# Norms at the boundaries of a two-block transformer kernel, and its last gate by token tiles

## The chip, the cores and the metric

The kernel runs on one core of a Trainium2 chip. The metric is the device time of one execution, in microseconds (us). The engines are TensorE (PE in the profile; PEld is its weight load), VectorE (DVE), ScalarE (ACT), GpSimd (POOL) and SyncE (SP), which issues most of the DMA transfers. Each engine works through its own instructions in order; semaphores tie the engines together.

## The reference

Two models in a row work on 512 tokens of width 1024, all in float32. The first has two layers, each with a mixer and a feed-forward network; a norm stands ahead of each of them and another on what it gives:

```python
h = x
for layer in range(2):
    xn = _rms_norm(h, norm_g[layer, 0])
    m = _even_mixer(xn, ...) if layer == 0 else _sgu_mixer(xn, ...)
    h = h + _rms_norm(m, norm_g[layer, 1])
    f = _squared_relu_mlp(_rms_norm(h, norm_g[layer, 2]), ffn_w1[layer], ffn_w2[layer])
    h = h + _rms_norm(f, norm_g[layer, 3])
```

with `_rms_norm(x, g) = x * rsqrt(mean(x * x) + eps) * g`, the mean over the 1024 columns of a token. The second model is one block whose shifts, scales and gates (`mod`) come from a condition vector: a norm, a scale and a shift, an attention mixer, a gate, `h = h + gate * mixer`; then a norm, a scale and a shift, a SwiGLU network, a gate, `h = h + gate * swiglu`; and a final norm with weights of its own. The kernel returns that.

## The kernel before

The residual stream `h` lies in SBUF with a token on each partition: four token tiles `i` of 128 tokens, 1024 columns each. The input `x` of a product lies the other way round, with features on the partitions, so between two blocks the tokens have to be normed and turned by TensorE (`fl`, L560, four 128x128 transposes into one PSUM bank). A float32 product is made of three matmuls (`mm3`, L275): every operand is split into a high part rounded to the matmul's format and the low part that is left (for weights L265 on ACT gives `whi` and L266 on DVE gives `wlo`, 1024 columns at a time).

There are five boundaries, near 319 us (even mixer to first feed-forward), 683 (first feed-forward to gMLP mixer), 964 (gMLP to second feed-forward), 1326 (second feed-forward to attention) and 1699 (attention to SwiGLU). `boundary` (L588) weaves three streams together on TensorE: `tail`, the last matmuls of the old block, token tile by token tile in two halves `c` of 512 columns; `bridge` or `shifted`, which turn two token tiles (half 0 is tiles 0 and 1, half 1 is tiles 2 and 3); and `head`, the first matmuls of the new block. The table `PLACES` (L229) says after how many steps of `tail(2)`, `tail(3)`, `head(0)` and `head(1)` which half is turned: an entry is (steps, half).

`norm_evac` (L530) is what follows each tail bank at the first four boundaries: `m` plus the bank on DVE (L540; a copy on ACT, L542, at the first), its sum of squares on ACT (L492, `ssm`), the product with the norm's weights on POOL (L544, in place), and after the second half the inverse root (L502 on DVE, L503 on POOL, `rsm`) and `h` (L548 on DVE, 1024 columns). `normed` (L523) then takes the sum of squares of the new `h` (`ssh`) and its inverse root (`col`). `bridge` evacuates unscaled transposes (L486 on ACT, L487 on DVE), and a later product applies the root; its broadcast over the partitions is `rb`. `shifted`, at the last two boundaries, needs the scaled token, since a shift is added: there L528 on ACT writes `h` times its root to another tile, that tile is turned, and for each of eight feature blocks ACT (L584) writes the high part of `x` from PSUM, DVE (L583) the whole value, and DVE (L585) the low part.

The SwiGLU network (L1593) runs in six hidden groups. `fi(g)` computes group `g`; `accum_group` (L1169) multiplies group `g-1` by its part of the output weights and adds the result to `m`, in eight banks, all four token tiles of `c` = 0 and then those of `c` = 1. After the loop the gate's row is made (`mod_row`, L511: matmuls `mrow` and copies on ACT), and POOL multiplies `m` by it (L1622) and adds it to `h` (L1623). The sixth group is the final tail: for each of its eight banks (`l`) DVE multiplies by the row (L1628, into `m`) and adds to `h` (L1629), ACT squares, POOL multiplies by the final norm's weights (L1631, into `m`), and after the second half of a tile the inverse root and the scaled output follow (DVE's half is L1637), and its transfer. A PSUM tag has two banks (`g`, `o`) or four (`s`). A Tile scheduler sets the order in which an engine gets its instructions, by priority and readiness.

## Time and profile before

| | |
|---|---|
| times of three runs | 2090.65, 2093.2, 2094.97 us (median 2093.2) |
| profiled execution | 2088.22 us, its span 2086.4 us |
| mean granted TensorE clock | 0.986 |
| TensorE busy | 2029.1 us (97%) |
| DVE, ACT, POOL busy | 53%, 39%, 9% |

The profile shows one execution. The span runs from its first to its last instruction. A busy TensorE is not a TensorE at full speed: its granted clock is one of two levels, 2.4 GHz (1.00) and 1.2 GHz (0.50), and a stretch's mean lies between them. Time in which an engine stands idle is put down to what released it, "idle before <- releaser".

### The profile page before, as it was taken

What the parts mean: (1) busy time and instruction counts of PE and PEld (TensorE: products, weight loads), DVE (VectorE), ACT (ScalarE), POOL (GpSimd) and SP (SyncE); (2) the same over time, 40 slices, a digit from 0 to 9 for tenths busy, and PEclk for the clock granted to TensorE, in tenths of its full rate; (3) what the DMA queues carried; (4) which work ended last, traced back from release to release, by engine and by line L of the source; (5) the groups of instructions that cost most, each with busy time, mean ns of one, the idle gap of its engine ahead of it and who ended that gap; (6) DMA issues with size and microseconds to landing.
All of it is one profiled execution on the core that took longest, in us unless ns stands there. A gap on an engine that the chain in (4) does not pass through costs nothing.

```text
span 2086.4 us, 25962 instructions
## 1 busy us (share of the span) xinstructions
PE 2029.1 (97%) x10296; PEld 1713.9 (82%) x10296; DVE 1110.1 (53%) x1682; ACT 810.9 (39%) x1356; POOL 184.0 (9%) x222
## 2 busy tenths in 40 slices
PE   8989999999999999999999999899999999999996
PEld 6867889888888788888888888898888888888885
DVE  7676646666665446665444444633563664334333
ACT  5455555322334443224523223534755344322221
POOL 3212230000002000003000000200000000000006
PEclk9989999999999999999999999999999999999998
DMA  7201044755542323221332233132122223232311
GB/s 250 84 31 41 31 154 125 241 190 195 178 144 68 125 89 100 89 90 61 121 101 91 91 101 101 51 102 71 60 73 65 77 92 119 93 101 92 100 61 41
DMA packets 59690, 213.54 MB, mean 102 GB/s; under 512 B 6951, under 2 KB 7272, under 8 KB 59184
## 3 DMA queue, kind: packets, MB, share of 16 engines
q1 hardware_dynamic: 56592, 202.84, 30.0%
q0 software_dynamic: 1728, 5.28, 0.9%
q10 hardware_dynamic: 1248, 3.76, 0.6%
q8 instruction: 81, 1.33, 0.3%
q14 instruction: 41, 0.34, 0.0%
HBM read 206.59 MB, written 2.10 MB: 100 GB/s over the span
## 4 chain that ended last, share of the span: by engine, by line
PE 77%; POOL 3%; DVE 3%; issue 2%; ACT 2%; POOLq 0%; ACTq 0%
PE g L278 12%; PE g L280 12%; PE g L279 12%; PE a L280 7%; PE a L279 7%; PE a L278 7%; PE h L279 2%; PE h L278 2%; PE h L280 2%; PE t L278 2%; PE t L279 2%; PE t L280 2%; POOL a L544 1%; PE l L278 1%; PE l L280 1%
## 5 line engine op out<-in xcount | busy, mean ns | idle before, releaser
L265 ACT CAST whi<-wraw 128x1024 fp32r<-128x1024 f32 x326 | 340.8, 1047 | 853.0 <-PE g L279 385.3
L266 DVE TENSOR_TENSOR wlo<-wraw,whi 128x1024 fp32r<-128x1024 f32 x326 | 399.3, 1228 | 312.9 <-ACT whi L265 309.5
L278 PE MATMUL g<-a,whi 128*128 128x512 f32 x1200 | 473.4, 395 | 0.0
L280 PE MATMUL g<-a,wlo 128*128 128x512 f32 x1200 | 470.1, 392 | 0.0
L279 PE MATMUL g<-a,whi 128*128 128x512 f32 x1200 | 469.8, 392 | 0.0
L278 PE MATMUL a<-whi,a 128*128 128x512 f32 x688 | 268.2, 390 | 0.0
L279 PE MATMUL a<-wlo,a 128*128 128x512 f32 x688 | 267.7, 389 | 0.0
L280 PE MATMUL a<-whi,a 128*128 128x512 f32 x688 | 267.7, 389 | 0.0
L280 PEld LDWEIGHTS g<-a,wlo 128*128 128x128 f32 x1200 | 225.9, 188 | 46.6
L278 PEld LDWEIGHTS g<-a,whi 128*128 128x128 f32 x1200 | 226.3, 189 | 45.4 <-DVE a L1575 0.2
L279 PEld LDWEIGHTS g<-a,whi 128*128 128x128 f32 x1200 | 226.2, 188 | 45.4
L1182 DVE TENSOR_TENSOR a<-a,a 128x512 f32<-128x512 f32 x168 | 114.6, 684 | 107.0 <-PE a L280 106.5
L279 PEld LDWEIGHTS a<-wlo,a 128*128 128x128 f32 x688 | 129.2, 188 | 26.8
L280 PEld LDWEIGHTS a<-whi,a 128*128 128x128 f32 x688 | 129.1, 188 | 26.7
L278 PEld LDWEIGHTS a<-whi,a 128*128 128x128 f32 x688 | 129.2, 188 | 26.5
L278 PE MATMUL h<-a,whi 128*128 128x256 f32 x384 | 108.6, 289 | 8.6 <-ACT a L584 5.2
L279 PE MATMUL h<-a,whi 128*128 128x256 f32 x384 | 109.1, 285 | 1.1 <-DVE a L585 1.1
L280 PE MATMUL h<-a,wlo 128*128 128x256 f32 x384 | 108.3, 284 | 0.0
L278 PE MATMUL l<-whi,a 128*128 128x512 f32 x256 | 101.6, 397 | 6.1 <-DVE a L1628 6.1
L1150 DVE SCALAR_TENSOR_TENSOR r<-g,rbc 128x512 f32<-128x512 f32 x52 | 35.9, 691 | 129.1 <-PE g L280 129.1
L280 PE MATMUL l<-whi,a 128*128 128x512 f32 x256 | 100.5, 393 | 0.0
L279 PE MATMUL l<-wlo,a 128*128 128x512 f32 x256 | 100.5, 393 | 0.0
(411 smaller groups left out, 2797.6 us busy)
## 6 DMA issues: line engine op xcount, KB each, us to landing
wraw<-wbig SPq DMA_DIRECT2D x320, 512.0 KB, 3.6
wada<-wada SPq DMA_DIRECT2D x48, 512.0 KB, 4.4
cw<-cmp_w SPq DMA_DIRECT2D x2, 1024.0 KB, 10.3
rowng<-rows POOLq DMA_DIRECT2D x4, 512.0 KB, 5.5
h<-x ACTq DMA_DIRECT2D x1, 2048.0 KB, 11.7
out<-a SPq DMA_DIRECT2D x8, 256.0 KB, 2.1
xin<-xT SPq DMA_DIRECT2D x3, 512.0 KB, 7.8
qt<-qt ACTq DMA_DIRECT2D x12, 128.0 KB, 2.3
```

Of the source, the lines that this page charges most:

```text
L265: nc.scalar.copy(hi[:, :w], raw)
L266: nc.vector.tensor_tensor(lo[:, :w], raw, hi[:, :w].bitcast(F32), ALU.subtract)
L278: mm(out, s[0], m[0], start=start, stop=False)
L279: mm(out, s[0], m[1], start=False, stop=False)
L280: self.gemm = mm(out, s[1], m[0], start=False, stop=stop).ins
L544: nc.gpsimd.tensor_tensor(t, t, g[:, c * 512:c * 512 + 512], ALU.mult)
L1150: done = nc.vector.scalar_tensor_tensor(r, o, 0.0, rb, ALU.max, ALU.mult).ins
L1182: nc.vector.tensor_add(t, t, o)
```

## The change

1. `norm_evac`: the product with the norm's weights of the second half (`c` = 1) goes to a tile of its own, `mg`, with a raised scheduling priority, where it was made in place; the update of `h` becomes two instructions of 512 columns.
2. `shifted`: the unscaled `h` is turned; L528 is gone. The inverse root is broadcast over the partitions by two small matmuls (`rb`) and copied to SBUF by ACT (`shb`). For each feature block DVE multiplies the transposed values by the weight and by `shb`, ACT adds the shift and writes the high part, DVE writes the low part; each reads what the one before it wrote. The first three of a half's four transposes are issued ahead of the broadcast, the fourth later.
3. `PLACES`: the gMLP boundary and the two shifted ones have other numbers.
4. The last gate: 16 products and 16 sums of 512 columns on POOL (`gated`) follow the accumulation of the last `accum_group`, bank by bank. The gate's row is made before `fi(0)`.

```diff
 PLACES = {
-    "norm": ((), ((2, 0),), ((18, 1), (34, 0)), ((20, 1),)),
-    "shifted": ((), ((12, 0),), ((27, 1),), ()),
+    "ffn": ((), ((2, 0),), ((18, 1), (34, 0)), ((20, 1),)),
+    "sgu": ((), ((2, 0),), ((23, 1), (30, 0)), ((20, 1),)),
+    "shifted": ((), ((0, 0), (7, 0), (14, 0)), ((16, 1), (25, 1), (40, 1)), ()),
 }
...
         self.factor(st["col"][:, i:i + 1], st["ssh"][:, i:i + 1])
-        if st["src"] is not self.h:
-            self.nc.scalar.activation(st["src"][:, i], self.h[:, i], AF.Copy, scale=st["col"][:, i:i + 1])
...
             self.square_sum(ss[:, 2 * i + c:2 * i + c + 1], t)
-            nc.gpsimd.tensor_tensor(t, t, g[:, c * 512:c * 512 + 512], ALU.mult)
             if c:
+                with self.tc.high_priority(URGENT):
+                    mg = self.rows.tile([P, 512], F32, tag="mg", name="mg", bufs=2)
+                    nc.gpsimd.tensor_tensor(mg, t, g[:, 512:], ALU.mult)
                 self.factor(rs[:, i:i + 1], ss[:, 2 * i:2 * i + 1], ss[:, 2 * i + 1:2 * i + 2])
-                h = self.h[:, i]
-                nc.vector.scalar_tensor_tensor(h, m[:, i], rs[:, i:i + 1], h, ALU.mult, ALU.add)
+                for k, t in enumerate((m[:, i, :512], mg)):
+                    h = self.h[:, i, 512 * k:512 * k + 512]
+                    nc.vector.scalar_tensor_tensor(h, t, rs[:, i:i + 1], h, ALU.mult, ALU.add)
                 self.normed(st, i)
+            else:
+                nc.gpsimd.tensor_tensor(t, t, g[:, :512], ALU.mult)
...
-        for k, o in self.flipped(st, half):
+        first = list(self.flipped(half, 0, 6))
+        yield
+        o = self.bank(self.ps, "rb", "s")
+        self.col_to_bc(o[:, :256], st["col"][:, 2 * half:2 * half + 2])
+        b = self.rows.tile([P, 256], F32, tag="shb", name="shb")
+        nc.scalar.copy(b, o[:, :256])
+
+        def evac(k, o):
             s = self.mod[:, sh * 8 + k:sh * 8 + k + 1]
             t = self.rows.tile([P, 256], F32, tag="sh", name="sh", bufs=2)
-            nc.vector.tensor_scalar(t, o, g[:, k:k + 1], s, ALU.mult, ALU.add)
-            nc.scalar.activation(x[0][:, k, t0:t1], o, AF.Identity, bias=s, scale=g[:, k:k + 1])
-            nc.vector.tensor_tensor(x[1][:, k, t0:t1], t, x[0][:, k, t0:t1].bitcast(F32), ALU.subtract)
+            nc.vector.scalar_tensor_tensor(t, o, g[:, k:k + 1], b, ALU.mult, ALU.mult)
+            nc.scalar.activation(x[0][:, k, t0:t1], t, AF.Identity, bias=s)
+            nc.vector.scalar_tensor_tensor(x[1][:, k, t0:t1], t, s, x[0][:, k, t0:t1].bitcast(F32), ALU.add, ALU.subtract)
+
+        for k, o in first:
+            evac(k, o)
+        yield
+        for k, o in self.flipped(half, 6, KD):
+            evac(k, o)
         yield
...
+            row, fin = self.mod_row(40, wk), self.row("nfin")
+
+            def gated(i, c):
+                cs = slice(c * 512, c * 512 + 512)
+                nc.gpsimd.tensor_tensor(m[:, i, cs], m[:, i, cs], row[:, cs], ALU.mult)
+                nc.gpsimd.tensor_tensor(self.h[:, i, cs], self.h[:, i, cs], m[:, i, cs], ALU.add)
+
             y = fi(0)
             for g in range(1, 6):
                 yn = fi(g)
-                self.accum_group("fo", y, m, g == 1)
+                self.accum_group("fo", y, m, g == 1, gated if g == 5 else None)
                 y = yn
-            row, fin = self.mod_row(40, wk), self.row("nfin")
             ss, col = self.cols4("ssm"), self.cols4("col")
-            for i in range(NT):
-                nc.gpsimd.tensor_tensor(m[:, i], m[:, i], row, ALU.mult)
-                nc.gpsimd.tensor_tensor(self.h[:, i], self.h[:, i], m[:, i], ALU.add)
```

`accum_group` calls `then(i, c)` behind each of its adds. Line numbers in the changed kernel are larger by 2 to 20.

On POOL, the end of the program: the gate's products and sums, the final norm's products (L1631), and its inverse roots (L503). Before:

```order
177 L1622 TENSOR_TENSOR a_13957<-a_13957,row_15872 128x1024 x2
178 L1623 TENSOR_TENSOR h<-h,a_13957 128x1024 x2
179 L1622 TENSOR_TENSOR a_13957<-a_13957,row_15872 128x1024 x2
180 L1623 TENSOR_TENSOR h<-h,a_13957 128x1024 x2
181 L1631 TENSOR_TENSOR a_13957<-h,rownfin 128x512
```

After (the last pairs of sixteen operations alike):

```order
202 L1638 TENSOR_TENSOR a_14001<-a_14001,row_14002 128x512
203 L1639 TENSOR_TENSOR h<-h,a_14001 128x512
204 L1638 TENSOR_TENSOR a_14001<-a_14001,row_14002 128x512
205 L1639 TENSOR_TENSOR h<-h,a_14001 128x512
206 L1653 TENSOR_TENSOR a_14001<-h,rownfin 128x512 x2
```

Product and sum alternate, one pair for each bank of 512 columns, and the final norm's first two products stand behind the last pair.

On POOL, the last token tiles at the gMLP boundary: L544, and after the change L554 (`c` = 0) and L547 (`c` = 1), are the products with the norm's weights, L503 and L505 the roots, L508 and L510 the transfer of a later norm's weights. Before:

```order
138 L544 TENSOR_TENSOR a_3530<-a_3530,rowng_5615 128x512 x2
139 L503 TENSOR_TENSOR rsm<-fa,mhalf 128x1
140 L503 TENSOR_TENSOR col<-fa,mhalf 128x1
141 L544 TENSOR_TENSOR a_3530<-a_3530,rowng_5615 128x512 x2
142 L508 DMA rowng_7695<-rows 128x1024
143 L503 TENSOR_TENSOR rsm<-fa,mhalf 128x1
144 L503 TENSOR_TENSOR col<-fa,mhalf 128x1
```

After:

```order
141 L554 TENSOR_TENSOR a_3538<-a_3538,rowng_5623 128x512
142 L547 TENSOR_TENSOR mg<-a_3538,rowng_5623 128x512
143 L505 TENSOR_TENSOR rsm<-fa,mhalf 128x1
144 L505 TENSOR_TENSOR col<-fa,mhalf 128x1
145 L547 TENSOR_TENSOR mg<-a_3538,rowng_5623 128x512
146 L554 TENSOR_TENSOR a_3538<-a_3538,rowng_5623 128x512
147 L510 DMA rowng_7711<-rows 128x1024
148 L505 TENSOR_TENSOR rsm<-fa,mhalf 128x1
149 L505 TENSOR_TENSOR col<-fa,mhalf 128x1
```

For the last token tile the product of `c` = 1 now stands ahead of that of `c` = 0, and the root behind both.

On DVE, the same place: from the update of `h` for the third token tile (L548, L551) over the evacuation of the first half's transposes (L487, L489) to the adds of the last token tile's two banks (L540). Before:

```order
623 L548 SCALAR_TENSOR_TENSOR h<-a_3530,rsm,h 128x1024
624 L487 SCALAR_TENSOR_TENSOR a_5654<-fl_95_5789,vecs,a_5653 128x256
625 L487 SCALAR_TENSOR_TENSOR a_5654<-fl_95_5798,vecs,a_5653 128x256
626 L487 SCALAR_TENSOR_TENSOR a_5654<-fl_95_5807,vecs,a_5653 128x256
627 L487 SCALAR_TENSOR_TENSOR a_5654<-fl_95_5816,vecs,a_5653 128x256
628 L540 TENSOR_TENSOR a_3530<-a_3530,l_95_5785 128x512
629 L500 TENSOR_SCALAR fa<-ssh 128x1
630 L487 SCALAR_TENSOR_TENSOR a_5654<-fl_95_5798,vecs,a_5653 128x256
631 L487 SCALAR_TENSOR_TENSOR a_5654<-fl_95_5807,vecs,a_5653 128x256
632 L487 SCALAR_TENSOR_TENSOR a_5654<-fl_95_5816,vecs,a_5653 128x256
633 L540 TENSOR_TENSOR a_3530<-a_3530,l_95_5838 128x512
```

After:

```order
629 L551 SCALAR_TENSOR_TENSOR h<-mg,rsm,h 128x512
630 L489 SCALAR_TENSOR_TENSOR a_5662<-fl_95_5803,vecs,a_5661 128x256
631 L489 SCALAR_TENSOR_TENSOR a_5662<-fl_95_5812,vecs,a_5661 128x256
632 L489 SCALAR_TENSOR_TENSOR a_5662<-fl_95_5821,vecs,a_5661 128x256
633 L502 TENSOR_SCALAR fa<-ssh 128x1
634 L489 SCALAR_TENSOR_TENSOR a_5662<-fl_95_5830,vecs,a_5661 128x256
635 L489 SCALAR_TENSOR_TENSOR a_5662<-fl_95_5803,vecs,a_5661 128x256
636 L489 SCALAR_TENSOR_TENSOR a_5662<-fl_95_5812,vecs,a_5661 128x256
637 L489 SCALAR_TENSOR_TENSOR a_5662<-fl_95_5821,vecs,a_5661 128x256
638 L489 SCALAR_TENSOR_TENSOR a_5662<-fl_95_5830,vecs,a_5661 128x256
639 L540 TENSOR_TENSOR a_3538<-a_3538,l_95_5799 128x512
640 L540 TENSOR_TENSOR a_3538<-a_3538,l_95_5852 128x512
```

Both adds stand behind all eight evacuations; at the second feed-forward boundary the order is the same.

On ACT, the attention boundary, from the square of the last bank of the third token tile (L492, L494): L528 is the scaling, L584 and L596 the high part of `x`, L590 the copy of the broadcast, L265 and L267 casts of weights. Before:

```order
739 L492 ACTIVATE junk,ssm<-a_8315 128x512
740 L265 CAST whi_10538<-wraw_10537 128x1024
741 L265 CAST whi_10692<-wraw_10691 128x1024
742 L492 ACTIVATE junk,ssh<-h 128x1024
743 L265 CAST whi_10723<-wraw_10722 128x1024
744 L528 ACTIVATE a_8315<-h,col 128x1024
745 L492 ACTIVATE junk,ssm<-a_8315 128x512
746 L584 ACTIVATE a_10282<-fl_207_10443,mod,mg 128x256
747 L265 CAST whi_10905<-wraw_10904 128x1024
748 L492 ACTIVATE junk,ssm<-a_8315 128x512
749 L584 ACTIVATE a_10282<-fl_207_10443,mod,mg 128x256
```

After:

```order
735 L494 ACTIVATE junk,ssm<-a_8339 128x512 x2
736 L267 CAST whi_10571<-wraw_10570 128x1024
737 L494 ACTIVATE junk,ssh<-h 128x1024
738 L590 COPY shb<-rb_10474 128x256
739 L267 CAST whi_10717<-wraw_10716 128x1024
740 L494 ACTIVATE junk,ssm<-a_8339 128x512
741 L596 ACTIVATE a_10306<-sh,mod 128x256 x2
742 L267 CAST whi_10761<-wraw_10760 128x1024
743 L267 CAST whi_10943<-wraw_10942 128x1024
744 L596 ACTIVATE a_10306<-sh,mod 128x256 x2
```

The copy stands behind the square of the third tile's `h` (`ssh`), and the first evacuation behind a cast and one more square.

## Rows read from the trace of the kernel before

**Rows 1.** The page, engines: busy us, share of span, instructions.

```profile
PE 2029.1 (97%) x10296; PEld 1713.9 (82%) x10296; DVE 1110.1 (53%) x1682; ACT 810.9 (39%) x1356; POOL 184.0 (9%) x222
```

**Rows 2.** Waits of TensorE: waiter, releaser, total us, times, longest.

```profile
PE l L278 <- DVE a L1628: 6.1, 1, 6.1
PE h L278 <- ACT a L584: 5.2, 1, 5.2
PE fl L560 <- DVE h L548: 5.1, 3, 3.8
...
PE h L278 <- DVE a L540: 1.3, 1, 1.3
...
PE h L279 <- DVE a L585: 1.1, 2, 0.6
```

**Rows 3.** POOL timeline, last gate: start, duration, work, idle before.

```profile
2043.35 4.74 POOL L1622 TENSOR_TENSOR a<-a,row 128x1024 f32<-128x1024 f32 x2 [336.28 <-ACT row L517]
2048.05 4.75 POOL L1623 TENSOR_TENSOR h<-h,a 128x1024 f32<-128x1024 f32 x2
2052.76 5.66 POOL L1622 TENSOR_TENSOR a<-a,row 128x1024 f32<-128x1024 f32 x2
...
2063.03 1.26 POOL L1631 TENSOR_TENSOR a<-h,rownfin 128x512 f32<-128x512 f32 x1
```

**Rows 4.** DVE timeline, last gate and final norm.

```profile
2038.18 0.69 DVE L1182 TENSOR_TENSOR a<-a,a 128x512 f32<-128x512 f32 x1 [2.03 <-PE a L280]
2040.90 0.69 DVE L1182 TENSOR_TENSOR a<-a,a 128x512 f32<-128x512 f32 x1 [2.03 <-PE a L280]
2050.48 0.69 DVE L1628 TENSOR_TENSOR a<-l,row 128x512 f32<-128x512 f32 x1 [8.90 <-POOL h L1623]
...
2053.98 2.17 DVE L1629 TENSOR_TENSOR h<-h,a 128x512 f32<-128x512 f32 x1
...
2066.07 0.49 DVE L1637 TENSOR_SCALAR a<-a,col 128x512 f32<-128x512 f32 x1 [8.25 <-POOL a L1631]
...
2078.33 0.68 DVE L1628 TENSOR_TENSOR a<-l,row 128x512 f32<-128x512 f32 x1
```

**Rows 5.** Windows: length, PE, PEld, DVE, ACT, POOL busy, PEclk, DMA.

```profile
682.80:686.00 3.20, 3.18 (x16) 3.18 (x16) 2.25 (x5) 2.51 (x6) 0.54 (x1) 0.50 0.96 319
...
2040.47:2042.37 1.90, 1.90 (x18) 1.86 (x16) 0.69 (x1) 0.58 (x1) 0.00 (x0) 1.00 0.00 0
...
2061.70:2067.80 6.10, 0.02 (x1) 0.00 (x0) 1.70 (x4) 1.27 (x3) 4.90 (x5) 0.67 0.17 66
2067.80:2073.40 5.60, 5.49 (x12) 3.80 (x12) 3.85 (x7) 2.16 (x7) 2.98 (x4) 0.50 0.25 95
```

**Rows 6.** DVE timeline, gMLP boundary, last token tile.

```profile
676.17 2.66 DVE L266 TENSOR_TENSOR wlo<-wraw,whi 128x1024 fp32r<-128x1024 f32 x2
...
678.87 2.16 DVE L266 TENSOR_TENSOR wlo<-wraw,whi 128x1024 fp32r<-128x1024 f32 x1
681.48 1.28 DVE L548 SCALAR_TENSOR_TENSOR h<-a,rsm,h 128x1024 f32<-128x1024 f32 x1 [0.46 <-POOL rsm L503]
```

**Rows 7.** POOL timeline, the same stretch.

```profile
677.82 2.12 POOL L544 TENSOR_TENSOR a<-a,rowng 128x512 f32<-128x512 f32 x1 [1.22 <-ACT junk L492]
```

**Rows 8.** ACT timeline, the same stretch.

```profile
677.03 0.62 ACT L492 ACTIVATE junk<-a 128x512 bf16<-128x512 f32 x1
```

**Rows 9.** DVE timeline, second feed-forward boundary.

```profile
961.66 1.65 DVE L487 SCALAR_TENSOR_TENSOR a<-fl,vecs,a 128x256 fp32r<-128x256 f32 x4
963.23 0.68 DVE L540 TENSOR_TENSOR a<-a,l 128x512 f32<-128x512 f32 x1
...
965.06 0.68 DVE L540 TENSOR_TENSOR a<-a,l 128x512 f32<-128x512 f32 x1
```

**Rows 10.** ACT timeline, attention boundary.

```profile
1323.65 1.15 ACT L528 ACTIVATE a<-h,col 128x1024 f32<-128x1024 f32 x1 [0.28 <-POOL col L503]
...
1325.32 0.55 ACT L584 ACTIVATE a<-fl,mod,mg 128x256 fp32r<-128x256 f32 x1
```

More of the change, by code (lines that the diff above doesn't have):

```diff
@@ L559, in flipped @@
                     c = (2 * k + j) * P
-                    self.mark = self.nc.tensor.transpose(o[:, c:c + P], st["src"][:, 2 * half + j, (k0 + k) * P:(k0 + k + 1) * P],
+                    self.mark = self.nc.tensor.transpose(o[:, c:c + P], self.h[:, 2 * half + j, (k0 + k) * P:(k0 + k + 1) * P],
                                                          self.ident).ins
@@ L567, in bridge @@
         t0, t1 = HALVES[half]
-        for k, o in self.flipped(st, half):
+        for k, o in self.flipped(half, 0, KD):
             self.scaled(x, o, k, self.vec(nxt, k), t0, t1)
@@ L1141, in ffn @@
             outs, head = self.head("w1", x, more=("w1",) * 2)
-            self.boundary(tail, lambda i: self.bridge(st, x, f"ng{l}2", rb, i), head, PLACES["norm"])
+            self.boundary(tail, lambda i: self.bridge(st, x, f"ng{l}2", rb, i), head, PLACES["ffn"])
             m = self.tokens()
@@ L1163, in ffn @@
                 done = after
[L1164 removed]
+            st, evac = self.norm_evac(m, f"ng{l}3", True)
             ws = [[self.unit("w2") for _ in range(2)] for c in range(2)]
@@ L1167, in ffn, with accum_group @@
         return tail, st
-    def accum_group(self, tag, y, m, first):
+    def accum_group(self, tag, y, m, first, then=None):
         nc = self.nc
@@ L1182, in accum_group @@
                     nc.vector.tensor_add(t, t, o)
+                if then is not None:
+                    then(i, c)
     def modulation(self, step):
@@ L1212, in sgu @@
             outs, head = self.head("sv", x, tm=True)
-            self.boundary(tail, lambda i: self.bridge(st, x, "ng10", rb, i), head, PLACES["norm"])
+            self.boundary(tail, lambda i: self.bridge(st, x, "ng10", rb, i), head, PLACES["sgu"])
             ws = vp.tile([P, 8, P], F32, name="ws")
@@ L1579, in mixer2 @@
         self.wide = True
-        st = {"ssh": self.cols4("ssh"), "col": self.cols4("col"), "src": self.tokens()}
-        row = self.mod_row(16)
+        st = {"ssh": self.cols4("ssh"), "col": self.cols4("col")}
+        row, m = self.mod_row(16), self.tokens()
         def evac(i, c, o):
             h = self.h[:, i, c * 512:c * 512 + 512]
-            t = st["src"][:, i, c * 512:c * 512 + 512]
+            t = m[:, i, c * 512:c * 512 + 512]
             nc.vector.tensor_tensor(t, o, row[:, c * 512:c * 512 + 512], ALU.mult)
```

10 lines of the change are left out of this document (4 added, 6 removed).

## The prediction

> **What bounds the kernel now.** First the page's busy times: TensorE is busy 2029.1 us of the 2086.4 us span [rows 1], so everything that this change can win lies in the 57.3 us in which TensorE stands still, and in stretches in which its granted clock is the lower of its two levels. Next the table of what TensorE waits for [rows 2]. Five of its rows belong to code that the change touches: 6.1 us in one piece for a DVE write of `a` in the last gate, 5.2 us in one piece for the ACT evacuation at the attention boundary (`h` waits for L584), 5.1 us for L548 before transposes (the longest 3.8), 1.3 us for L540 and 1.1 us for L585. Together they are 18.8 us. The rest of the 57.3 is other code, and the stretch after the last matmul: the window that begins at 2067.80 has TensorE busy to its end at about 2073.3 [rows 5], so 13.1 us of the span follow it. The profiled execution took 2088.22 us, 1.8 more than its span, and the median of the three runs is 2093.2, 5 us above it; I take differences from the trace and set them off from the median.
>
> **The end: the gate by tiles.** The POOL timeline [rows 3] shows the mechanism. The last matmuls of the accumulation feed the add at 2040.90 [rows 4]; POOL starts only at 2043.35, when the gate row is there, and does eight operations of 1024 columns in four pairs, of which the first three took 4.74, 4.75 and 5.66 us; the first product of the final norm (L1631) comes at 2063.03. The DVE timeline [rows 4] shows who waits: the first L1628 at 2050.48 has 8.90 us of idle before it, and DVE stands again before 2066.07. TensorE runs on while it finds free PSUM banks, stops at 2061.70, and restarts at 2067.80 [rows 5] with a granted clock of 0.50, the 1.2 GHz level, where at 2040.47, busy without a break, it had 1.00. It needs 5.49 us for twelve matmuls there. The last L1628 comes at 2078.33, and 8.07 us later the span ends.
>
> After the change the gate is sixteen products and sums of 512 columns, each pair behind the accumulation add of its own bank. The adds of two neighbouring banks are at 2038.18 and 2040.90 [rows 4], so a bank of 12 matmuls takes 2.72 us and one matmul 0.227. A POOL pair of 512 columns takes two times 1.27: half of the 2.37 us for 1024 [rows 3] is 1.19, and the 512-wide product at 2063.03 took 1.26. So 2.55 us of POOL work arrive every 2.72 us, and the last pair ends some 2.6 us after the last add (2040.90 + 0.69), at about 2044.2. The first bank of the final tail is full 2.72 us after 2042.37, at 2045.1, and finds its gate done. DVE then needs per token tile two L1628 (0.69), two L1629 and one L1637 (0.49 [rows 4]), less than the 5.44 us that two banks take, so the tail stays behind TensorE alone. It has 96 matmuls, 21.8 us at 0.227 from 2042.37 on: the last ends at about 2064.3, its L1628 starts at 2064.4 rather than at 2078.33, and the 8.07 us after it stay. **Term: -13.9 us.** The row's own products (`mrow`, 1.90 us of TensorE [rows 5]) move from before the final tail to before the hidden layer; they are paid there instead, between matmuls that keep TensorE full, so they cancel. A cover is needed for one thing: POOL work beside the accumulation adds. The add reads PSUM and SBUF, as L1628 does, and the L1628 of 2050.48 took 0.69 in the middle of a POOL sum [rows 3, 4]; I cost it at nothing.
>
> Bounds: if each gate operation were stretched to the 2.12 us of the POOL product at 677.82 [rows 7], sixteen would take 34 us and end at about 2056.7; this is a rival below. The other end is the whole 6.1 + the lower clock (5.49 for twelve matmuls against 2.72, 2.8) + the backlog that puts the last L1628 5.0 behind the last matmul: 13.9 again, so there is no more to gain here.
>
> **The product beside the square.** In the old order the second half's product (L544) works in place, so it waits for the square on ACT and the inverse root on POOL stands behind it: square 0.62 [rows 8], product 1.26 at best [rows 3], root, then L548 of 1.28 [rows 6]. With its own tile the product starts with the square and hides it, 0.6 us, and L548 in two halves lets the transposes of the first columns start 0.6 earlier. Taken alone that is 1.2 us for each chain on the path. But the rows before the gMLP boundary [rows 6, 7] show that the chain of the last token tile is not alone: L266 on DVE takes 2.66 for two pieces at 676.17 and 2.16 for one at 678.87, and the POOL product between them takes 2.12 instead of 1.26. The two engines take turns: the product, seen to start at 677.82, ends at 679.9, about 1.1 after the DVE pair at 678.8; then the L266 issued at 678.87 ends 1.1 after the product. In the new order POOL has, for this tile, the second half's product ahead of the first half's, and both stand ahead of the root; each takes its turn against one piece of L266. I get the first product done at 679.6, the second at 681.8, the row's DMA issue and the root by 683.3 and the first half of `h` at 684.0, where L548 ended at 682.76.
>
> The Trainium skill, "SBUF — State Buffer", section "Who interferes with whom", says that a DVE instruction with two SBUF inputs contends with a GpSimd instruction that reads SBUF, and that the one that comes second is blocked until the first is through. The turns in [rows 6, 7] agree with it, and by it the product gains nothing from an early start; without the rule the chain would end at about 681.6, 2.4 us sooner.
>
> **Five boundaries**, each by the place of TensorE that waits:
> - First feed-forward (near 319): one of the two short waits of transposes for L548 goes (5.1 - 3.8 is 1.3 for both [rows 2]), and a bank of the tail is read about as much later, since DVE has all evacuations of the first half ahead of it: 0, between -1 and +1.
> - gMLP (near 683): the later transposes stand nine matmuls, 2.04 us, further down, and the chain ends 1.2 later; the 3.8 us stall becomes about 3.0 and the lower clock behind it stays (0.50 from 682.80 to 686.00 [rows 5]): -1.0, between -3 and 0.
> - Second feed-forward (near 964): DVE does L540 of two banks between and behind seven small evacuations, the first at 963.23 and the second at 965.06 [rows 9]. The new order has all eight evacuations (1.65 for four) ahead of both. The first add is then about 2.0 later, the second 0.5 to 0.8 as it waits behind one more ACT cast. TensorE waits for these banks in one piece rather than two, and the next chain starts later: +1.3, between -0.5 and +2.2.
> - Attention (near 1326): the ACT scaling of 1.15 us [rows 10] goes, and the transposes read `h` itself. But the broadcast's copy stands on ACT behind the square of the third tile, and every evacuation behind that copy; three of the four transposes of a half come early, and the fourth stands on TensorE ahead of the last three matmuls of the tail. I get the first high part at 1324.5 where L584 ended at 1325.87 [rows 10], half a us of which the later fourth transpose takes back: -0.9, between -3 and +1.5.
> - SwiGLU (near 1699): almost nothing waited here (part of the 1.1 us of L585 [rows 2]). Now three steps in a row, DVE, ACT, DVE, stand where ACT and DVE read PSUM independently, behind the copy and two casts; the first low part comes about 0.9 later (the copy, of L584's size, 0.55 [rows 10], and one small evacuation, 0.41 [rows 9]), and four broadcast matmuls of half width add 0.5 (0.12 each, half of 0.227): +1.4, between -0.5 and +3.
>
> Sum of the boundaries +0.8; with the end -13.1. 2093.2 - 13.1 gives **2080.1 us** (and 2075.1 by the profiled execution).
>
> **The rivals.**
> (a) The forecast, 2080: end in full, boundaries about even.
> (b) The boundaries win too: products and scalings were on the path, the turns on the port are fewer than I drew, the stalls of 3.8 and 5.2 shrink to where the clock stays up. For it: 5.1 + 5.2 in [rows 2], each with a lower clock behind it. Against: the rows of the turns [rows 6, 7]. The lower ends of the five places sum to -8.0; most of it would give 2073.
> (c) POOL lags in the last gate, by 2.12 per operation, done at 2056.7. Two products of the final norm and a root (about 0.55, a short operation of POOL) later, at 2059.8, DVE gets past the first L1637, which now starts at 2066.07 [rows 4]; what follows is as now, and the end gives 6.3: 2088. Against it: the stretched product was one against a DVE operation with both inputs in SBUF, and the adds of the accumulation, which read PSUM, do not stretch POOL's work if L1628 is a guide.
> (d) Slower than before: the new wait of TensorE in its own order. The fourth transpose can only run when a bank is free, banks come free only behind the broadcast's copy, and the copy stands on ACT behind a square that waits for `h`. If this costs TensorE a stall like today's 5.2 us [rows 2] for each of two halves at two boundaries, and behind each 3.2 us at half the clock as after 682.80 [rows 5], 1.6 lost, that is 27.2 us where one such place, 6.8, is paid now: 20.4 added, and 2093.2 - 13.9 + 20.4 gives 2100. It decides from about 5.2 us a place, stall and clock together. Against it: the copy of the first half needs only the roots of the first two token tiles, which lie before the whole stretch.
> (e) The gain of the end is not there because the last banks wait for something else: the fin products and L1629 share POOL and DVE too. With 2.17 for a contended sum [rows 4] the tile needs 0.69 + 0.69 + 2.17 + 2.17 + 0.49 = 6.2 us against 5.44 of TensorE, 0.8 us each, 3 us in all: 2083. It lies inside the range.
>
> **How the numbers follow.** (a) with (e) 0.68, (b) 0.17, (c) 0.06, (d) 0.04, and 0.05 for a mix of them that ends within 0.2%, 4.2 us, which is about what a measurement of this kernel can tell from no change. The prediction is 2080. The five places' ends sum to -8.0 and +7.7 against +0.8; they will not all fall one way, so I take 7 below, to 2073, which takes in most of (b), and 8 above, to 2088, which takes in (c). Faster 0.91, within 0.2% 0.05, slower 0.04.
>
> **What would show it.** In the trace of the changed kernel: POOL pairs of about 2.55 us, one for every 2.72, in the last accumulation; no wait of TensorE in the final tail and a clock of 1.00 to its end; the span's end some 30 us after the last accumulation add, where it is 45.5 now (2086.4 - 2040.9). At the gMLP boundary the two POOL products in the new order, one of them stretched above 2 us; a stall of about 3 there; one stall of 2.5 to 3 at the second feed-forward boundary. At attention the copy `shb` behind the square. What would make the prediction wrong: an L1182 stretched above 0.69 beside POOL, a stall above 4 us with clock 0.50 at the SwiGLU boundary, or a chain at the gMLP boundary that ends before 682.

## The result and the profile after

The changed kernel takes 2073.33 us, the median of four runs (2072.95 to 2074.83), where the kernel before took 2091.93 in the runs beside it (2089.79 to 2094.97). The ratio is 0.9911, 95% interval 0.9894 to 0.9929: 18.6 us faster, 15 to 22 by the interval. Its profiled execution took 2073.41 us, its span is 2071.6, 14.8 below the span of before, and the mean granted clock 0.990. The prediction was 2080 with a range of 2073 to 2088, so the time lies at the range's lower edge.

What TensorE waits for in the profile after, in the columns of [rows 2]:

```profile
PE fl L565 <- DVE h L551: 4.5, 2, 3.4
PE h L280 <- DVE a L540: 2.7, 1, 2.7
...
PE h L281 <- DVE a L597: 2.0, 2, 1.3
...
PE fl L565 <- ACT shb L590: 1.3, 1, 1.3
...
PE h L280 <- ACT a L596: 0.6, 1, 0.6
```

The 6.1 us for the last gate are gone, and the 5.2 us in one piece at the attention boundary have become four shorter waits, of 1.26, 0.62, 1.27 and 1.13 (the last is the shorter of the two for L551). The end, on POOL (the columns of [rows 3]):

```profile
2023.26 1.28 POOL L1638 TENSOR_TENSOR a<-a,row 128x512 f32<-128x512 f32 x1 [317.82 <-DVE a L1200]
2024.62 1.28 POOL L1639 TENSOR_TENSOR h<-h,a 128x512 f32<-128x512 f32 x1
...
2043.52 1.28 POOL L1638 TENSOR_TENSOR a<-a,row 128x512 f32<-128x512 f32 x1
2044.88 1.28 POOL L1639 TENSOR_TENSOR h<-h,a 128x512 f32<-128x512 f32 x1
2046.79 1.29 POOL L1653 TENSOR_TENSOR a<-h,rownfin 128x512 f32<-128x512 f32 x1 [0.63 <-DVE h L1651]
```

and on DVE (as [rows 4]):

```profile
2030.32 2.06 DVE L268 TENSOR_TENSOR wlo<-wraw,whi 128x1024 fp32r<-128x1024 f32 x1 [1.76 <-ACT whi L267]
2032.30 0.67 DVE L1200 TENSOR_TENSOR a<-a,a 128x512 f32<-128x512 f32 x1
...
2041.47 0.69 DVE L1200 TENSOR_TENSOR a<-a,a 128x512 f32<-128x512 f32 x1 [2.03 <-PE a L282]
2044.26 0.69 DVE L1650 TENSOR_TENSOR a<-l,row 128x512 f32<-128x512 f32 x1 [2.10 <-PE l L282]
...
2063.59 0.68 DVE L1650 TENSOR_TENSOR a<-l,row 128x512 f32<-128x512 f32 x1
```

Each pair of product and sum takes 2.6 us on POOL (there are eight pairs, sixteen operations in all; the description of the change counts twice as many), the last add of the accumulation (L1200) still takes 0.69 beside them, and the first product of the final tail (L1650, at 2044.26) waits for its matmuls and for nothing else. The last one comes at 2063.59, 0.4 us behind the last matmul. The windows (as [rows 5]) give the clock of four stretches:

```profile
685.20:688.40 3.20, 3.20 (x22) 2.95 (x23) 2.85 (x6) 2.50 (x7) 0.54 (x1) 1.00 0.59 196
964.30:968.30 4.00, 4.00 (x19) 4.00 (x20) 4.00 (x5) 2.68 (x6) 3.35 (x2) 0.50 0.34 101
1325.40:1330.00 4.60, 4.60 (x38) 4.60 (x39) 4.45 (x9) 2.67 (x7) 1.87 (x2) 1.00 0.24 89
2041.50:2063.00 21.50, 21.50 (x96) 17.65 (x94) 13.79 (x21) 6.52 (x15) 13.80 (x13) 1.00 0.13 50
```

TensorE is busy through the whole final tail at a clock of 1.00, where [rows 5] had a stop of 6.1 us and 0.50 behind it. At the gMLP and attention boundaries the clock is 1.00 as well; at the second feed-forward boundary it is 0.50. The kernel before had 1.00 behind its stops at the second feed-forward boundary and 0.50 behind that at the attention boundary:

```profile
966.00:970.00 4.00, 4.00 (x35) 4.00 (x35) 4.00 (x4) 1.23 (x3) 2.47 (x3) 1.00 0.42 131
1325.90:1328.00 2.10, 2.04 (x7) 1.74 (x8) 2.10 (x5) 1.46 (x2) 0.95 (x1) 0.50 0.93 265
```

To see where the 14.8 us went, I took the start of every DVE and ACT instruction that both traces have, and the median of the differences (after minus before) in stretches of 25 us between the places that the change touches:

| place | forecast | change of the difference in this place |
|---|---|---|
| even mixer, untouched | 0 | +1.4 |
| first feed-forward boundary | 0 | -0.6 |
| gMLP boundary | -1.0 | -2.7 |
| second feed-forward boundary | +1.3 | +2.4 |
| attention boundary | -0.9 | -2.4 |
| SwiGLU boundary | +1.4 | +0.6 |
| the row of the last gate, in front of the hidden layers | paid there | +1.8 |
| last gate and final norm, to the span's end | -13.9 with the row | -15.4 |
| sum | -13.1 | -14.8 |

### The profile page after: what moved, and what is told of

It is laid out like the page before. It is cut to its first block, busy times and chain, and to the rows that moved or that the text cites. A ratio compares the mean times of both kernels' runs of the same rounds, so it can differ in the third digit from the quotient of the medians.

```text
span 2071.6 us, 26020 instructions
## 1 busy us (share of the span) xinstructions
PE 2026.2 (98%) x10312; PEld 1713.2 (83%) x10312; DVE 1113.7 (54%) x1698; ACT 801.9 (39%) x1352; POOL 189.5 (9%) x230
## 3 DMA queue, kind: packets, MB, share of 16 engines
q8 instruction: 81, 1.33, 0.3%
## 4 chain that ended last, share of the span: by engine, by line
PE 90%; DVE 4%; POOL 3%; ACT 2%; issue 1%; DMA 0%; POOLq 0%; SPq 0%; ACTq 0%; DVEq 0%
PE g L280 13%; PE g L282 13%; PE g L281 13%; PE a L282 8%; PE a L280 8%; PE a L281 8%; PE h L281 2%; PE h L280 2%; PE h L282 2%; PE t L280 2%; PE t L281 2%; PE t L282 2%; PE l L280 2%; PE l L282 2%; PE l L281 2%
## 5 line engine op out<-in xcount | busy, mean ns | idle before, releaser
L267 ACT CAST whi<-wraw 128x1024 fp32r<-128x1024 f32 x326 | 340.9, 1048 | 851.3 <-PE g L281 385.3
L1200 DVE TENSOR_TENSOR a<-a,a 128x512 f32<-128x512 f32 x168 | 114.4, 684 | 104.1 <-PE a L282 103.6
## 6 DMA issues: line engine op xcount, KB each, us to landing
h<-x ACTq DMA_DIRECT2D x1, 2048.0 KB, 11.3
```

The costliest lines, as they stand in the source:

```text
L267: nc.scalar.copy(hi[:, :w], raw)
L1200: nc.vector.tensor_add(t, t, o)
```

## The experiments

They start from the table above: nearly the whole gain is the last gate; the boundaries are worth two or three us together, and the product in its own tile is worth nothing at the boundaries where weight casts stand in its way. Each expectation says what its Theory A and its rival are.

**The last gate alone** (`gate_only`) is the kernel before with the fourth part of the change, as in the diff of the change; **the boundaries alone** (`no_gate`) is the changed kernel without it.

> The kernel before with the last gate by token tiles alone. Theory A (the trace's ledger: 15.3 us from the stretch after the hidden layers, 1.8 us paid for the gate's row ahead of them): 13.5 us faster than before, ratio 0.9935, and the clock after each boundary as before. Rival B (the end and the boundaries share the gain; the end only looks large because earlier stages shifted it): under 10 us faster.

> The changed kernel with the last gate as before: boundaries alone. Theory A: the five boundaries sum to -2.7 us (-0.6, -2.7, +2.4, -2.4, +0.6), ratio 0.9987. Rival B (the medians, 18.6 us apart, are right and the two profiled executions, 14.8 apart, are not): -5 us or more, ratio 0.9976 or less.

Measured: 2076.34 (2075.0 to 2078.27, five runs), ratio 0.9932 (0.9919 to 0.9946), 14.2 us faster by the ratio; and 2088.49 (2085.63 to 2090.28, eleven runs), ratio 0.9988 (0.9979 to 0.9997), 2.5 us faster. The two sum to 16.7, within the 15 to 22 of the whole. In the trace of `gate_only`, from the last gate to the end, the difference to before changes by -15.4, as in the changed kernel, and the boundaries' waits are those of [rows 2]:

```profile
PE h L278 <- ACT a L584: 5.2, 1, 5.2
PE fl L560 <- DVE h L548: 5.1, 3, 3.9
```

Theory A holds for both; Rival B of each falls. What `gate_only` does not separate are the two things that it changes: the row is made early, and the gate is split by banks. In [rows 3] POOL's first product waits for the row (336.28 us, <-ACT row L517) and not for the accumulation. An estimate from [rows 3, 4]: with the row at hand the old operations of 1024 columns could have begun when the first token tile had its last add, three banks of 2.72 before the one that ends at 2041.59, so at about 2033.4, and at their 19.7 us together (2043.35 to 2063.03) they would have been done at about 2053. The final tail's seventh bank, the first of the last token tile, is full at about 2061.4 in the kernel before (seven times 2.72 behind 2042.37), or 2059.5 without `mrow`. So the early row alone may bring most of the 14 us; no run shows how much of it the split by banks is worth.

The windows of `no_gate` show something that neither expected:

```profile
684.67:687.90 3.23, 3.23 (x18) 3.03 (x19) 2.88 (x6) 2.53 (x7) 0.54 (x1) 0.69 0.66 204
1326.00:1330.00 4.00, 3.85 (x18) 3.85 (x19) 4.00 (x8) 2.27 (x5) 1.39 (x1) 0.50 0.34 119
```

Its boundaries are those of the changed kernel instruction for instruction, TensorE stopped before the first stretch for 3.37 us as it did there for 3.36 (and before the second for 0.89, where it was 1.27), and yet the clock behind the stops is 0.69 and 0.50, not 1.00. The gMLP boundary is worth -1.5 here and the attention boundary -1.6, a us less each than in the changed kernel's profile, and the five boundaries of this one execution sum to -0.7; the -2.5 is that of the medians.

**The product in place** (`inplace`): the changed kernel with the old lines of `norm_evac`.

```diff
+            nc.gpsimd.tensor_tensor(t, t, g[:, c * 512:c * 512 + 512], ALU.mult)
             if c:
-                with self.tc.high_priority(URGENT):
-                    mg = self.rows.tile([P, 512], F32, tag="mg", name="mg", bufs=2)
-                    nc.gpsimd.tensor_tensor(mg, t, g[:, 512:], ALU.mult)
                 self.factor(rs[:, i:i + 1], ss[:, 2 * i:2 * i + 1], ss[:, 2 * i + 1:2 * i + 2])
...
+                h = self.h[:, i]
+                nc.vector.scalar_tensor_tensor(h, m[:, i], rs[:, i:i + 1], h, ALU.mult, ALU.add)
```

> The changed kernel with the norm's product in place behind the square and h in one update, as before. Theory A (at the gMLP and the second feed-forward boundary the product in its own tile stands ahead of the other half's product and takes turns with weight casts, so the last token tile's chain ends 1.5 us later there): these two boundaries gain 1 to 2 us each, the attention boundary loses under 1; 2071 to 2072, 1 to 3 us faster than the changed kernel. Rival B (the product beside the square is what shortened the gMLP and attention stalls): 2 to 3 us slower than the changed kernel, and the stop of 3.8 us with clock 0.50 behind it is back at the gMLP boundary.

Measured: 2070.24 (2069.02 to 2073.31, four runs), ratio 0.9905 (0.9891 to 0.9918). The runs alone hardly tell it from the changed kernel's 0.9911; the traces do. What TensorE waits for with the product in place:

```profile
PE fl L560 <- DVE h L548: 2.5, 3, 1.9
...
PE h L281 <- DVE a L592: 1.7, 2, 1.0
...
PE h L280 <- DVE a L540: 1.3, 1, 1.3
...
PE fl L560 <- ACT shb L585: 1.2, 1, 1.2
```

The gMLP stop is 1.9 instead of 3.4, and the second feed-forward boundary has its two short stops back instead of one of 2.7. By the differences of starts the gMLP boundary is worth -4.6 and the second feed-forward +0.6, 3.6 us better than in the changed kernel together; the attention boundary is 1.3 worse in this execution, at a clock of 0.50, where under 1 was expected. POOL shows why the first two are better. In the changed kernel, at the gMLP boundary:

```profile
677.37 3.27 POOL L547 TENSOR_TENSOR mg<-a,rowng 128x512 f32<-128x512 f32 x1 [2.67 <-DVE a L540]
680.61 2.24 POOL L554 TENSOR_TENSOR a<-a,rowng 128x512 f32<-128x512 f32 x1
...
683.78 0.57 POOL L505 TENSOR_TENSOR rsm<-fa,mhalf 128x1 f32<-128x1 f32 x1
```

and with the product in place:

```profile
675.18 1.31 POOL L544 TENSOR_TENSOR a<-a,rowng 128x512 f32<-128x512 f32 x1 [0.21 <-ACT junk L494]
677.70 2.16 POOL L544 TENSOR_TENSOR a<-a,rowng 128x512 f32<-128x512 f32 x1 [1.21 <-ACT junk L494]
...
680.79 0.57 POOL L505 TENSOR_TENSOR rsm<-fa,mhalf 128x1 f32<-128x1 f32 x1
```

In place the first half's product began before the casts of weights came and took 1.31, as in the open; only the second waited for them (2.16). In the changed kernel both met them, 3.27 and 2.24, and the root started 3.0 us later by the two traces' own times, of which 1.0 is that the changed kernel's execution ran that much behind before it came to this boundary: 2.0 for the order, of which 1.5 reached TensorE. Theory A holds on the mechanism. This run also isolates the place of the transposes at this boundary, since everything else there is as before: nine matmuls moved ahead of them took the stop from 3.85 to 1.85, about nine times 0.227. That is 2.0 of the 4.6; the rest is the clock behind the stop, 1.00 here where [rows 5] has 0.50 from 682.80 to 686.00:

```profile
682.70:686.00 3.30, 3.26 (x22) 3.01 (x23) 2.95 (x7) 3.23 (x9) 0.54 (x1) 1.00 0.97 318
```

**The old evacuation at the shifted boundaries** (`shifted_old`): the changed kernel with L528, L583 to L585 and the old numbers.

```diff
-    "shifted": ((), ((0, 0), (7, 0), (14, 0)), ((16, 1), (25, 1), (40, 1)), ()),
+    "shifted": ((), ((12, 0),), ((27, 1),), ()),
...
+        if st["src"] is not self.h:
+            self.nc.scalar.activation(st["src"][:, i], self.h[:, i], AF.Copy, scale=st["col"][:, i:i + 1])
```

> The changed kernel with the scaling on ACT, the scaled tokens turned, and the old places at the attention and SwiGLU boundaries. Theory A (turning the unscaled tokens took the 2.4 us at the attention boundary and cost 0.6 at the SwiGLU boundary): 1.8 us slower than the changed kernel; at attention one stop of about 5 us with clock 0.50 behind it. Rival B (the third tile's chain, shortened by the product beside the square, took it): the attention boundary stays as in the changed kernel, and the whole is 0.6 faster.

Measured: 2074.15 (2072.74 to 2074.83, four runs), ratio 0.992 (0.9907 to 0.9934), 0.8 above the changed kernel's median, not told apart from it by the runs. In the trace:

```profile
PE h L280 <- ACT a L591: 3.8, 1, 3.8
```

One stop of 3.8 at the attention boundary, not 5.2, and a time 0.8 above rather than 0.6 below: neither theory holds as it stands. The 1.4 between 5.2 and 3.8 belong to the new `norm_evac`, since nothing else in the code of this boundary differs from the kernel before: the third tile's second product starts on POOL at 1317.36, with no cast in its way, beside its square, where in the kernel before it starts at 1318.10, behind the square. That much is as Rival B says. That turning the unscaled tokens took any of the rest is not shown: TensorE's waits there sum to 4.3 in the changed kernel and 2.8 in `no_gate`, and by starts this boundary is worth -1.8 with the old evacuation and -2.4 or -1.6 with the new one (the changed kernel, `no_gate`). The share of the new evacuation there is not larger than what the clock does in one execution. At the SwiGLU boundary it costs what Theory A says: 0.0 by starts with the old evacuation, +0.6 with the new one in both of those traces.

**The adds first** (`add_first`, and `inplace_add_first` with the product in place):

```diff
             if acc:
-                nc.vector.tensor_add(t, t, o)
+                with self.tc.high_priority(URGENT):
+                    nc.vector.tensor_add(t, t, o)
```

> The changed kernel with the adds of the tail's banks (L540) at a raised priority: on DVE one of the two adds of the last tile comes four evacuations earlier, on POOL the first half's product stands again ahead of the second half's. Theory A (the order of these two is what made the last tile's chain 1.5 us later and the second feed-forward boundary 2.4 slower): the stops fall from 3.4 to about 2.4 at the gMLP boundary and from one of 2.7 to two of together 2; 2071 to 2072. Rival B (the product in its own tile meets the weight casts in whatever order): POOL's two products take 5.5 us together as before, 2073.

> The changed kernel with the product in place and the tail's adds at a raised priority. Theory A (the two stops of 1.1 and 1.3 us at the second feed-forward boundary wait for the adds behind evacuations): they shrink to under 1.5 together, 2069. Rival B (the first low part of x is then later and TensorE waits for that): 2070.

Measured: 2071.88 (2071.62 to 2072.94, five runs), ratio 0.9908 (0.9893 to 0.9922), and 2073.06 (2069.1 to 2074.07, five runs), ratio 0.9909 (0.9892 to 0.9925). The first did on POOL what it should:

```profile
676.13 1.30 POOL L555 TENSOR_TENSOR a<-a,rowng 128x512 f32<-128x512 f32 x1 [2.28 <-ACT junk L494]
677.38 2.28 POOL L548 TENSOR_TENSOR mg<-a,rowng 128x512 f32<-128x512 f32 x1
```

The first half's product is back ahead of the casts (1.30, then 2.28), and the gMLP stop fell from 3.4 to 1.8. Theory A holds there: the order of the two products, not the tile of its own, cost the 1.5 us. At the second feed-forward boundary the one stop became two of 1.2 and 1.6, not less together, and the clock behind them was 0.50 again (+2.6 by starts), so nothing was won. The second was a miss: on DVE a cast of weights slid between the two adds,

```profile
960.95 0.68 DVE L541 TENSOR_TENSOR a<-a,l 128x512 f32<-128x512 f32 x1
...
962.78 2.09 DVE L268 TENSOR_TENSOR wlo<-wraw,whi 128x1024 fp32r<-128x1024 f32 x1
964.79 0.68 DVE L541 TENSOR_TENSOR a<-a,l 128x512 f32<-128x512 f32 x1
```

and the second stop grew from 1.3 to 2.6 us; the gMLP stop grew as well, from 1.85 to 2.45. Rival B named another cause, and the time is not told apart from the changed kernel's either.

**Two halves in place** (`inplace_split`): as `inplace`, with `h` updated in two instructions.

> The changed kernel with the product in place, but h updated in two halves of 512 columns. Theory A (the halves alone let the first transposes of the last tiles start 0.6 us earlier, and the product's own tile was what cost time): the stop at the gMLP boundary 1.2 instead of 1.85, 2069.5 to 2070.2. Rival B (two updates of 0.75 are longer than one of 1.28, and the square of h waits for both): 2070.5 to 2071.

Measured: 2071.38 (2070.76 to 2071.47, five runs), ratio 0.9903 (0.9886 to 0.9919). The gMLP stop is 1.74 instead of 1.85, not 1.2. The transposes do start behind the first half (at 683.15, the first update of 0.75 ending at 683.10 and the second at 683.76), as Theory A has it; but by the place of TensorE the update itself began 0.4 later than in `inplace`, since on DVE the last bank's add came 0.4 later, behind evacuations. What is left at that stop is 0.1 us, and the time is not told apart from that of `inplace`.

**The broadcast earlier** (`rb3`): as `inplace`, with

```diff
-    "shifted": ((), ((0, 0), (7, 0), (14, 0)), ((16, 1), (25, 1), (40, 1)), ()),
+    "shifted": ((), ((0, 0), (3, 0), (14, 0)), ((16, 1), (25, 1), (40, 1)), ()),
...
-        nc.scalar.copy(b, o[:, :256])
+        with self.tc.high_priority(URGENT):
+            nc.scalar.copy(b, o[:, :256])
```

> The changed kernel with the product in place, and at the shifted boundaries the broadcast of the roots four steps of the tail earlier, so that its copy stands on ACT ahead of the square of the third tile. Theory A (the copy behind the square held the fourth transpose for 1.2 us and the first evacuations): no stop before the fourth transpose, low parts a us earlier; 1 to 2 us faster than with the product in place alone, 2068.5 to 2069.5. Rival B (the evacuations stand on DVE behind the update of the third tile's h and a weight cast anyway): the stop moves to the first high part, no change, 2070.

Measured: 2065.56 (2065.22 to 2066.75, four runs), ratio 0.9877 (0.986 to 0.9894), 3 us below what Theory A expected. On ACT in the changed kernel:

```profile
1320.08 1.06 ACT L494 ACTIVATE junk<-h 128x1024 bf16<-128x1024 f32 x1 [2.58 <-DVE h L551]
...
1321.13 0.35 ACT L590 COPY shb<-rb 128x256 f32<-128x256 f32 x1
```

and here:

```profile
1315.45 0.36 ACT L586 COPY shb<-rb 128x256 f32<-128x256 f32 x1
1318.13 1.06 ACT L494 ACTIVATE junk<-h 128x1024 bf16<-128x1024 f32 x1 [2.31 <-DVE h L548]
```

The copy (`shb`) is done 2.3 us before the square that it stood behind, TensorE no longer stops before the fourth transpose, one stop of 1.2 is left in front of the first high part, and the clock behind it is 1.00. This is the price of the in-order wait that rival (d) of the prediction named, taken away: the medians of `inplace` and `rb3` are 4.7 us apart. By starts, 3.7 of it lie at the attention boundary (-4.75 against -1.02 to the kernel before), with the clock of 1.00 against 0.50 included. TensorE's waits there are 1.23, 0.61 and 0.99 in place, 2.8 together, and one of 1.19 in `rb3`: 1.6 is what the order gives in stops, and most of the rest of the 3.7 is the clock. It is more than this pair of executions: with the copy behind the square this boundary is worth between -0.8 and -2.4 in the six traces that have it so, and in `rb3_sgu27`, below, -4.8 again at a clock of 1.00. The edit moves the broadcast and raises the copy's priority; which of the two did it, no run shows.

**The gMLP transposes further down** (`rb2_sgu27`, `rb3_sgu27`): `rb3` with the first of the gMLP numbers at (27, 1) instead of (23, 1), in the first of the two also the broadcast at (2, 0).

> The changed kernel with the product in place, the broadcast five steps of the tail earlier at the shifted boundaries, and the last tiles' transposes at the gMLP boundary six matmuls further down. Theory A (each stop is as long as the matmuls that could stand ahead of it are missing): the gMLP stop of 1.85 falls by 6 times 0.227 to 0.5, the attention stop of 1.2 before the first high part by the weight cast of 1.2 that now follows the first evacuations on DVE; 1.5 to 2.5 us faster than with the broadcast four steps earlier, 2063 to 2064. Rival B (the second half of the gMLP head then waits for the evacuation of these transposes): a new stop of about 1.4 behind the row's broadcast there, 2065.

> As the version with the broadcast four steps earlier, with the last tiles' transposes at the gMLP boundary six matmuls further down: the two moves that held, together. Theory A (the gMLP stop falls from 1.85 to 0.5 as in the version before, the attention boundary keeps one stop and its clock): 2064 to 2064.5, 1.4 faster than 2065.6. Rival B (which boundaries lose clock is drawn anew in each execution, and 2065.6 had the better draw): 2066 to 2068 for both.

Measured: 2067.8 (2066.8 to 2068.29, four runs), ratio 0.9888 (0.9872 to 0.9905), and 2063.84 (2062.89 to 2065.89, four runs), ratio 0.9876 (0.9859 to 0.9892). The gMLP stop is 0.49 and 0.50 in their traces, six matmuls less than 1.85, as expected. By starts the boundary gains 0.7 of it (-5.3 in both, -4.6 in `rb3`): a stop of 0.4 is new before the root's broadcast (`rb`), near where Rival B of the first expected one of 1.4. With the broadcast at (2, 0) the attention boundary has stops of 0.26, 0.95 and 0.68, and loses its clock:

```profile
684.00:687.00 3.00, 2.97 (x20) 2.45 (x20) 2.65 (x6) 2.93 (x8) 0.54 (x1) 1.00 1.00 348
...
1319.40:1324.00 4.60, 3.89 (x20) 3.69 (x21) 4.60 (x10) 4.41 (x10) 2.53 (x3) 0.68 0.32 108
```

so it is worth -2.9 there, 1.9 less than in `rb3`. It misses its 2063 to 2064: its median is 2.2 us above that of `rb3` in spite of the smaller gMLP stop, but the two intervals overlap, and the attention mixer, which no edit touches, alone took 1.5 more in its trace than in that of `rb3`. `rb3_sgu27` has the lowest time of all: its interval, 0.9859 to 0.9892, ends below where the changed kernel's begins, 0.9894, and its median is 9.5 us below the changed kernel's and 27 below that of the kernel before beside it (2091.08). The time is the one Theory A expected, but it is not told apart from `rb3` (0.986 to 0.9894). Of its profiled execution 3.0 us belong to no edit: in the attention mixer, which none of these kernels changes, the clock stayed at 1.00,

```profile
1425.00:1450.00 25.00, 24.34 (x195) 23.30 (x196) 9.33 (x16) 12.93 (x31) 0.00 (x0) 1.00 0.20 64
1450.00:1475.00 25.00, 23.90 (x160) 19.30 (x159) 13.50 (x29) 16.12 (x50) 0.64 (x1) 1.00 0.21 65
```

where in the execution of the kernel before it did not:

```profile
1425.00:1450.00 25.00, 24.23 (x183) 23.09 (x182) 10.95 (x19) 12.05 (x31) 0.00 (x0) 0.92 0.27 86
1450.00:1475.00 25.00, 23.90 (x175) 21.42 (x174) 11.93 (x20) 13.26 (x51) 0.00 (x0) 0.94 0.14 43
```

## Why the prediction was right, and where its sizes were off

- **The end** was forecast at -13.9 with the row paid elsewhere. Measured: -15.4 and +1.8, -13.6; alone, 14.2 faster (11.3 to 16.9). The steps hold one by one: pairs of 2.6 for 2.55 forecast, no wait in the final tail, clock 1.00, adds of 0.69 beside POOL. One step was off without harm: a cast of weights on DVE (2.06 at 2030.32) held one add back to 2032.30, so POOL fell behind and its last pair ended at 2046.2, not 2044.8 (the forecast's 2044.2 and the 0.6 by which this execution ran late); the final tail's first L1651 met that pair and took 1.73, and only the final norm's first product behind it came later. What the forecast did not separate is the split by banks from the row made early, which alone, by the estimate under `gate_only`, would let the old operations start some 10 us sooner.
- **Rival (c)** did not come: the sixteen operations took 1.28 to 1.30 per operation throughout. **Rival (e)** came in small: a token tile of the final tail takes about 5.65 us by the starts of L1659 (2050.55, 2056.20, 2061.86) against 5.44 of TensorE, and all of it together put the last L1650 0.4 behind.
- **The gMLP boundary**: the chain was forecast 1.2 later and the stop 3.0; measured, the first half of `h` ended 1.5 later (685.14 less the 0.85 by which this execution ran late there, against 682.76) and the stop was 3.4. The term was mis-sized because I let the lower clock stay; it was 1.00 in the changed kernel and 0.67 to 0.69 in two other executions of the same code. So of the -2.7 only 0.5 is the stop (3.85 to 3.36).
- **The second feed-forward boundary**: +1.3 forecast, +2.4 to +2.6 measured in every execution with the product in its own tile. The stop in one piece is there, 2.7, but it costs nothing by itself: TensorE's waits there sum to 3.0, and to 3.1 in the kernel before (1.12, 1.33, 0.65). What I left out is the clock of 0.50 behind it, and that is where the loss comes from.
- **The attention boundary**: -0.9 forecast, -2.4 and -1.6 measured. The first high part ended at 1323.45, 1.0 before the 1324.5 that I had drawn, or 1.5 with the 0.5 by which this execution ran late; TensorE then stopped 1.27 for the first low part, which I had not drawn. Its waits fell from 5.8 (5.20 and 0.56) to 4.3 in all; the rest is again the clock, which the single stop of 5.2 had cost (0.50 from 1325.90) and which is 1.00 in the changed kernel's profile.
- **The SwiGLU boundary**: +1.4 forecast, +0.6 measured; the third step hid behind a weight cast: the first high part ended at 1696.97, and DVE was in a cast until 1697.89 before it wrote the low part.
- **The anchor.** The largest error is not in a term. The traces differ by 14.8 where I had 13.1, and the rest of the 6.7 us between 2080 and 2073.3 is that I set the difference off from the median of before, 2093.2, while the execution profiled took 2088.2. Over the runs beside the experiments the kernel before spreads from 2087.8 to 2095.6 with medians near 2091, and the changed kernel from 2073.0 to 2074.8; the changed kernel's profiled execution stands at its median, that of before 3 to 5 us below its own. That the time still fell into the range, 0.3 above its lower end, is in part luck: that end was drawn for rival (b), the boundaries' gain, and it was mostly the anchor that used it up.
- **Rival (b)**, the boundaries win too, had its share: -2.5 (0.6 to 4.4) by `no_gate`, not the -8. **Rival (d)** had the right place (the fourth transpose behind the copy, 1.3 us) and a quarter of its 5.2 us.

## What to carry to other kernels

Work that one engine does in a block between two phases of TensorE belongs behind each tile of the phase before, if the engine's time per tile is below TensorE's: 2.6 against 2.72 us per bank was enough for the block to vanish from TensorE's waits. Ask first, though, what the block waits for: here it was a row made late, and how much of the 13.6 us the early row would have taken alone was not measured. A step that is moved ahead on a shared resource has to be looked at with what then stands behind it: the earlier product at the gMLP boundary put two operations into the casts' way where one had been, and the same product in the old order won more. An in-order wait can be cut by issuing its producer earlier in the stream, as the broadcast four steps earlier, with priority for its copy, shows. A raised priority reorders other work too: for the adds it took 1.5 us off a stop in one kernel (`add_first`) and put 1.3 on another in the next (`inplace_add_first`).

## What the runs showed of the hardware that was not expected

- Whether the granted clock falls behind a stop is not settled by the stop's length. Behind 3.36 us it was 1.00 (changed kernel, gMLP), behind 3.37 us in the same code 0.69 (`no_gate`), behind 2.73 us 0.50. It falls without a stop too: in a stretch of the attention mixer that no edit touches, TensorE was busy for the whole of it in both executions, before

```profile
1560.00:1570.00 10.00, 10.00 (x57) 8.04 (x57) 5.56 (x14) 4.88 (x12) 0.00 (x0) 1.00 0.17 53
```

and in `gate_only`

```profile
1560.00:1570.00 10.00, 10.00 (x48) 8.02 (x47) 4.26 (x13) 4.08 (x9) 0.00 (x0) 0.83 0.18 53
```

The second lost 1.65 us there. Not every place is drawn anew: behind the stop of 2.73 at the second feed-forward boundary the clock fell in all three traces that have it (changed kernel, `no_gate`, `shifted_old`), and behind the gMLP stops of 1.74 to 2.45 it was 1.00 in all five (`inplace`, `add_first`, `inplace_add_first`, `inplace_split`, `rb3`). But one or two us at each of several places, different from one execution to the next, are the size of the kernel before's scatter, and a boundary's gain below 2 us can't be read from one trace unless the clock behind it is compared as well.

- POOL and DVE waited for each other when both read two operands from SBUF, but not always turn by turn. In the changed kernel at the gMLP boundary, DVE's rows beside the POOL rows shown with `inplace` are

```profile
677.14 2.35 DVE L268 TENSOR_TENSOR wlo<-wraw,whi 128x1024 fp32r<-128x1024 f32 x2
...
679.57 2.16 DVE L268 TENSOR_TENSOR wlo<-wraw,whi 128x1024 fp32r<-128x1024 f32 x1
```

The first row is two casts of weights, one behind the other, 2.35 us: neither is stretched (one takes 1.21 in the open, the third in `add_first`). POOL's product of 677.37 began during the first of them and ended at 680.64, through both, 3.27 us for an operation of 1.3. Only the third cast waited, for the product (2.16), and POOL's next product in turn for that cast (2.24). In `add_first`, where POOL's first product began ahead of the casts, the two engines did take turns of one instruction each: product, cast, product, cast. There the first product took 1.30 and the second 2.28, and the two casts 4.45 where the pair above took 2.35:

```profile
676.29 4.45 DVE L268 TENSOR_TENSOR wlo<-wraw,whi 128x1024 fp32r<-128x1024 f32 x2
```

The prediction drew turns of one instruction each for the changed kernel, which did not take them there, and came to the same place by luck: the second product done at 681.8, measured 682.85 less the 0.85 by which this execution ran late. The Trainium skill, "SBUF — State Buffer", section "Who interferes with whom", says that such a pair contends and that issue order decides who is blocked. `add_first` agrees; in the changed kernel the product that began at 677.37 was still blocked by the second cast, which began at 678.28. Why a cast got ahead of the waiting product in one and not in the other is open.
